# Attention on one core: keys of three head pairs loaded once and copied across the partitions by ScalarE, and the steps on y of branch B moved

## The chip, the cores and the metric

The kernel runs on one core of a Trainium2 chip. Its engines run their own instruction streams and wait for each other by semaphores: the PE (TensorE) multiplies, VectorE (DVE) and ScalarE (ACT) work on tiles element by element, GpSimd (POOL) and SyncE (SP) mostly issue DMAs here. The metric is the device time of one launch in microseconds, as the median of several runs.

## The reference

One layer of an encoder on 1024 tokens with 1024 features, in float32. The change lies in its middle part:

```python
u = rms_norm(h)
qA, kA, vA, qB, kB, vB, gA, gB = split(u @ W_in)
yA = neighbourhood_attention_2d(qA, kA, vA)      # 8 heads of 64, 8 rows x 16 columns around each query
yB = windowed_gqa_sink(rope(qB), rope(kB), vB)   # 8 query heads, 2 key heads, |i - j| <= 128, a sink logit
h = h + (sigmoid(gA) * (yA @ W_A) + sigmoid(gB) * (yB @ W_B)) @ W_out
```

Ahead of it and behind it stands a feed-forward half step of width 2816.

## The kernel before

Products in float32 are made of three matmuls on operands that are split in a high and a low part (`mm3`, L149, L153, L155). The dense products outside the attention work that way and take most of the time.

**The attention loop.** The loop at the end of the trunk goes through 64 units. Units 0 to 31 are branch B: eight blocks of 128 queries, four head pairs each. Units 32 to 63 are branch A: four head pairs `hp`, eight blocks each. The loop is pipelined over iterations n: `scores` of unit n (PE L1631 and L1632, VectorE L1636 adds the bias and takes the row's extreme, ScalarE L1639 takes the exp and the row's sum), `turn` of unit n-2 (transposes on the PE, L1654; ScalarE casts the result to a high part and VectorE subtracts it for the low part, L95 and L98), and `values` of unit n-3 (PE L1668 or L1673, then `write`: L1570 and L1573 for branch B, L1591, L1592, L1596 and L1598 for branch A). Twice in each iteration `filling` takes steps from the generator `filler`: matmuls of the gates (`gate`, copied out of PSUM at L1331 and stored to `g_d`), then the product of branch B's y with W_B (`branch_b`), then products of branch A. So the PE always has dense work between the small matmuls of the units, as long as what both need is there.

**Keys of branch A.** `prep_a(hp)` loads what a head pair needs; it is a generator that the loop drains twice per iteration from n = 23, 33, 41 and 49 on for pairs 0 to 3. K of each head, in a high and a low part, is wanted on both halves of the 128 partitions, and each half is loaded with a DMA of 256 KB on GpSimd's queue (L1303), eight per pair. Then come q (L1306) and v (L1313).

**y of branch B.** The exps are not normalised in the loop. Their sums are collected in `sums_b`; `inverse` (at n = 32) takes the reciprocal, transposes it, copies it out of PSUM (L1355) and writes it to `inv_d` in DRAM (L1356). y goes to DRAM too (`y_d`, one store for four units, L1573). `fetch_y(r0)` loads 128 rows of y (L1368) and calls `fetch_inverse`, which spreads the inverse sums over the partitions with two loads (L1360). `split_y` multiplies both (L1364) and splits the result (L95, L98) for `branch_b`. The dictionary of steps at the end of `filler` says at which step of the last gate each of these happens for the four row blocks.

**Gates of branch B.** `fetch_gate` loads a gate's row block from `g_d` on SyncE's queue (L1477), `open_gate` takes its tanh on ScalarE (L1486).

**What sets the order.** The code names the operations; a scheduler of the framework puts them in an order on each engine by its own estimate of when their inputs are ready, and may put an instruction several units ahead. On the chip each engine keeps that order. Tiles come from rotating buffers (four `raw`, two `xs`, eight `ws`, four banks each of the PSUM pools `d` and `g`), and a load into a buffer waits until its last reader is done.

Of the kernel before, what the change touches and what calls it, by code (L numbers as in the profile page):

```python
# [11 lines left out]
F32R = mybir.dt.float32r  # L12
# [3 lines left out]
P = 128  # L16
# [15 lines left out]
def f32v(ap):  # L32
    return ap.bitcast(F32)
# [3 lines left out]
def trunk_kernel(ctx, tc, x, xt, n1, wg1, wu1, wd1, nm, win, rpb, sink, wa, wb, wout,  # L37
                 n2, wg2, wu2, wd2, nf, c_rope, c_mask_a, c_mask_b, out):
    nc = tc.nc
# [14 lines left out]
    def nm_(s):  # L54
        uid[0] += 1
        return f"{s}_{uid[0]}"
# [12 lines left out]
    def new_fx(k, dt=F32):  # L69
        fx[k] = main.tile([P, 1024], dt, tag=f"fx{k}", bufs=1, name=nm_("fx"))  # L70
        return fx[k]

    def new_ar(g, dt=F32R):
        ar[g] = main.tile([P, 4, 1024], dt, tag=f"ar{g}", bufs=1, name=nm_("ar"))
        return ar[g]

    def slot(k):
        return ar[k // 4][:, k % 4, :]

    def bank(tag):  # L80
        return ps.tile([P, 512], F32, tag=tag, name=nm_(tag))

    def raw4():
        return main.tile([P, 1024], F32, tag="raw", bufs=4, name=nm_("raw"))

    def xs4():
        return main.tile([P, 1024], F32, tag="xs", bufs=2, name=nm_("xs"))
# [6 lines left out]
    def split(dst_hi, dst_lo, src, eng=None, late=False):  # L94
        hi = nc.scalar.copy(dst_hi, src)  # L95
        if late:
            pin(hi)
        (eng or nc.vector).tensor_tensor(dst_lo, src, f32v(dst_hi), op=ALU.subtract)  # L98
# [642 lines left out]
    for h in range(8):  # L741
        for e, f in ((2, bias_fetch), (5, bias_add), (10, bias_put)):
            k = e + 6 * h
# [321 lines left out]
    def by_block(a):  # L1065

        return a.rearrange("p (b j x) -> p j b x", b=NTT, x=16)

    def in_block(a):
        return a.rearrange("p (j b x) -> p j b x", b=NTT, x=16)  # L1070
# [98 lines left out]
    def halves(a):  # L1169
        return a[:HD], a[HD:]  # L1170
# [106 lines left out]
    heads_a = {}  # L1277
# [12 lines left out]
    def prep_a(hp):  # L1290

        slots = [slot(k) for k in ((12, 13, 14, 15, 20, 21) if hp % 2 == 0 else (22, 23, 8, 9, 10, 11))]
        qs, kd, kl = slots[0:2], slots[2:4], slots[4:6]

        def head(k, base, lo):

            r0 = (base + hp) * P + k * HD
            return zs_d[lo][r0:r0 + HD, :]

        for k in range(2):  # L1300
            for lo, dst in enumerate((kd, kl)):
                for a in halves(dst[k]):
                    nc.gpsimd.dma_start(a, head(k, 4, lo))  # L1303
                yield
            for lo in range(2):
                nc.gpsimd.dma_start(halves(qs[k])[k ^ lo], head(k, 0, lo))  # L1306
            yield
        va = [new_fx(k, F32R).rearrange("p (b d) -> p b d", d=P) for k in ((2, 3) if hp % 2 == 0 else (0, 1))]
        for k in range(2):
            src = v_d[hp % 2].rearrange("n t p (j m s x) -> m s j p (n t) x", j=2, m=2, s=2)[hp // 2, k]  # L1310
            dst = f32v(va[k]).rearrange("p (b j) x -> j p b x", j=2)
            for j in range(2):
                (nc.gpsimd if hp > 1 else nc.sync).dma_start(dst[j], src[j])  # L1313
        heads_a[hp] = (qs, kd, kl, va)

    def u_half(c, n):
        h, l = rhs(((B11, T4), (B21, B22))[c // 4][n])
# [16 lines left out]
    Y_B = (4, 5), (6, 7), (16, 17), (18, 19)  # L1334
# [14 lines left out]
    def inverse(t, r0):  # L1349

        n = t.shape[1]
        nc.vector.reciprocal(t, t)
        pt = bank("d")
        nc.tensor.transpose(pt[:n, :P], t, ident)
        nc.scalar.copy(inv_t[:n], pt[:n, :P])  # L1355
        nc.gpsimd.dma_start(inv_d[r0:r0 + n // NTT].rearrange("a (j t) -> (a j) t", t=P), inv_t[:n])  # L1356

    def fetch_inverse(r, r0):
        for s, a in enumerate(halves(r)):
            nc.gpsimd.dma_start(a, inv_d[r0 + s].partition_broadcast(HD))  # L1360
        return r

    def times(a, b):
        nc.vector.tensor_tensor(a, a, b, op=ALU.mult)  # L1364

    def fetch_y(r0):
        mix["y", r0] = raw4()
        nc.gpsimd.dma_start(mix["y", r0], y_d[r0:r0 + P, :])  # L1368
        mix["inv", r0] = fetch_inverse(raw4(), r0 // HD)

    def split_y(slots, r0, eng):

        h, l = [slot(k) for k in slots]
        r = mix.pop(("y", r0))
        times(r, mix.pop(("inv", r0)))
        if r0 < 512:
            r = in_block(r)
            h, l = by_block(h), by_block(l)
        split(h, l, r, eng, True)
# [95 lines left out]
    def fetch_gate(dc):  # L1475
        r = mix["rb", dc] = xs4() if dc % 3 else masks[:, :1024]
        nc.sync.dma_start(r, g_d[D + dc * P:D + (dc + 1) * P, :])  # L1477
# [6 lines left out]
    def open_gate(dc):  # L1484
        r = mix["rb", dc]
        pin(nc.scalar.activation(r, r, AF.Tanh, scale=0.5))  # L1486

    def branch_b():

        for g in (0, 6):  # L1490
            new_ar(g, F32)
        for dc in range(NC8):
            bs = [bank("g") for _ in range(2)]
            mm = branch_mm(bs, mix.pop(("w", dc)), Y_B)
            for c in range(4):
                drain(mm, 1)
                yield
                if c == (0 if dc else 2) and dc + 2 < NC8:
                    fetch_gate(dc + 2)
                if c == 0 and dc == 0:  # L1500
                    split_y(Y_B[3], 3 * P, nc.vector)
                if c == 1 and dc == 0:
                    open_gate(0)
                if c == 0:
                    if dc + 2 < NC8:
                        fetch_w(dc + 2)
                    else:
                        fetch_wa(0, dc + 2 - NC8)
                elif c == 3 and dc + 1 < NC8:
                    open_gate(dc + 1)  # L1510
            rb = mix.pop(("rb", dc))
            for n in range(2):
                sl = slice(n * 512, (n + 1) * 512)
                nc.vector.scalar_tensor_tensor(out=merged(dc)[:, sl], in0=rb[:, sl], scalar=1.0, in1=bs[n],
                                               op0=ALU.add, op1=ALU.mult)
# [14 lines left out]
    def filler():  # L1530
        for dc, nxt in zip(gates, gates[1:] + [None]):
            if nxt is not None:
                yield from gate(dc, {2: lambda: gate_load(gates.index(nxt))})
            else:
                yield from gate(dc, {0: lambda: [fetch_gate(0), fetch_w(0), fetch_w(1)],
                                     1: lambda: [fetch_y(c * P) for c in range(2)],
                                     2: lambda: fetch_y(2 * P),
                                     3: lambda: split_y(Y_B[0], 0, nc.vector),
                                     4: lambda: [split_y(Y_B[1], P, nc.vector), fetch_y(3 * P)],
                                     5: lambda: fetch_gate(1),  # L1540
                                     6: lambda: split_y(Y_B[2], 2 * P, nc.vector)})
        yield from branch_b()
        for k, p in (("P1", 0), ("P5", 0), ("P1", 1), ("P5", 1)):
            a_product(p, k)
            yield
            a_keep(p, k)
            if k == "P1" and p == 1:
                forms_last(0, "P6")
                forms_last(0, "P3")
            if p == 0 and k == "P5":  # L1550
                a_fetch(0)
        a_open(0)
# [139 lines left out]
    for n in range(1 << 30):  # L1692
        got = next(source, None)
        if got is not None:
            scores(got)
        pipe.insert(0, got)
        for hp, n0 in preps.items():
            if n == n0:
                prep = prep_a(hp)
        if prep:  # L1700
            drain(prep, 1)
        filling(n)
        if len(pipe) > 2 and pipe[2] is not None:
            turn(pipe[2])
        if prep:
            drain(prep, 1)
        if n >= 26 and (n - 26) % 8 == 0 and n < 58:
            fetch_bias((n - 26) // 8)
        if n == NTT * 4:
            inverse(sums_b, 0)  # L1710
        elif n in (NTT * 5, NTT * 6, NTT * 7):
            inverse(sums_a[n // NTT - 5], 2 * (n // NTT) - 2)
        if n in (57, 58, 60):
            fetch_ya(min(n - 57, 2))
        if n in (60, 61):
            forms_first(n - 60)
        if n == NTT * 8:
            for k in A_WEIGHTS:
                fetch_wa(*k)
        if n == 63:  # L1720
            times(mix["ya", 2], mix["inv_a", 2])
            form("P2", 0, mix["ya", 2][:, L])
        filling(n)
        if len(pipe) > 3 and pipe[3] is not None:
            values(pipe[3])
        pipe = pipe[:4]
        if not any(pipe):
            break
# [249 lines left out]
```

## Time and profile before

| | us |
|---|---|
| median of 3 runs | 1931.53 |
| lowest and highest run | 1928.98, 1934.27 |
| the profiled run: its own time | 1929.65 |
| the profiled run: its span | 1927.9 |
| mean clock granted to the PE | 0.995 of full speed |

The profile is that of one execution. An engine's line gives its busy time; the waits are idle times of an engine with the instruction that ended them; the chain goes back from the last instruction to what released each. The scores (L1631) stand between 916.6 and 1159.6 us of the span; branch A begins near 1022. Rows are shown in the prediction, where each is used.

### The profile page before, as it was taken

The numbers are of one execution on the slowest core, as the hardware profiler recorded it, in microseconds if no ns is written. First come the engines' busy times: TensorE is split into PE (matmuls) and PEld (weight loads), VectorE is DVE, ScalarE is ACT, GpSimd is POOL, SyncE is SP. The second block draws the span as 40 slices with busy tenths as digits, with TensorE's granted clock in tenths as the row PEclk, the third lists the DMA queues.
The fourth block names the chain that finished last, engine by engine and source line by source line (L and its number), as shares of the span: only waits on it lengthen the run. The fifth ranks groups of instructions, "written<-read, shape, count | busy, mean of one in ns | idle before, by whom it ended". The sixth has DMA issues, their size and how long they took to land.

```text
span 1927.9 us, 26104 instructions
## 1 busy us (share of the span) xinstructions
PE 1905.2 (99%) x9024; PEld 1597.0 (83%) x9024; DVE 1440.5 (75%) x2543; ACT 935.4 (49%) x1824; POOL 252.7 (13%) x471
## 2 busy tenths in 40 slices
PE   9999999999999999999998999999999999999998
PEld 7888888888888888898997888888888888888886
DVE  8988887868957877766776789879676566559664
ACT  7533554544446543445776676265333333344453
POOL 0011322210000112211112310010110001000010
PEclk9999999999999999999999999999999999999999
DMA  6256978887444277865549989653422322493341
GB/s 268 94 186 229 333 274 295 289 292 271 135 148 148 97 235 218 238 217 190 143 129 246 262 239 348 231 207 120 148 103 99 127 88 106 144 362 104 103 143 61
DMA packets 178213, 369.58 MB, mean 192 GB/s; under 512 B 18016, under 2 KB 76304, under 8 KB 178080
## 3 DMA queue, kind: packets, MB, share of 16 engines
q1 hardware_dynamic: 136784, 236.23, 37.1%
q0 software_dynamic: 40432, 130.63, 19.9%
q8 instruction: 71, 1.16, 0.3%
q10 hardware_dynamic: 864, 1.05, 0.2%
q14 instruction: 62, 0.51, 0.1%
HBM read 247.73 MB, written 121.88 MB: 192 GB/s over the span
## 4 chain that ended last, share of the span: by engine, by line
PE 95%; DMA 3%; DVE 1%; ACT 1%; issue 1%; POOL 0%; POOLq 0%; SPq 0%; ACTq 0%; DVEq 0%
PE g L149 17%; PE g L153 17%; PE g L155 17%; PE d L155 12%; PE d L149 12%; PE d L153 12%; PE d L1654 2%; DMA raw<-inv_d 1%; PE g L1673 1%; PE d L1631 1%; PE d L1632 1%; PE d L142 1%; DMA xs<-g_d 1%; PE g L1668 1%; DMA fx<-v_d 0%
## 5 line engine op out<-in xcount | busy, mean ns | idle before, releaser
L149 PE MATMUL g<-ar,ws 128*128 128x512 f32 x1062 | 407.8, 394 | 0.5 <-ACT xs L1331 0.5
L153 PE MATMUL g<-ar,ws 128*128 128x512 f32 x1062 | 404.1, 391 | 0.0
L155 PE MATMUL g<-ar,ws 128*128 128x512 f32 x1062 | 403.0, 391 | 0.0
L153 PE MATMUL d<-ar,ws 128*128 128x512 f32 x706 | 274.9, 389 | 0.6 <-DVE ar L1000 0.6
L149 PE MATMUL d<-ar,ws 128*128 128x512 f32 x706 | 275.3, 390 | 0.0
L155 PE MATMUL d<-ar,ws 128*128 128x512 f32 x706 | 275.0, 389 | 0.0
L155 PEld LDWEIGHTS g<-ar,ws 128*128 128x128 f32 x1062 | 199.8, 188 | 42.1
L153 PEld LDWEIGHTS g<-ar,ws 128*128 128x128 f32 x1062 | 199.7, 188 | 41.4 <-DVE ar L98 0.3
L149 PEld LDWEIGHTS g<-ar,ws 128*128 128x128 f32 x1062 | 196.5, 189 | 36.9 <-ACT xs L1331 0.8
L334 DVE TENSOR_TENSOR ws<-raw,ws 128x512 fp32r<-128x512 f32 x216 | 147.6, 689 | 77.4 <-ACT ws L327 76.5
L327 ACT CAST ws<-raw 128x512 fp32r<-128x512 f32 x216 | 132.7, 620 | 141.8 <-PE g L155 60.8
L153 PEld LDWEIGHTS d<-ar,ws 128*128 128x128 f32 x706 | 132.6, 188 | 28.7 <-DVE ar L1000 1.3
L155 PEld LDWEIGHTS d<-ar,ws 128*128 128x128 f32 x706 | 132.5, 188 | 28.2 <-DVE ws L334 0.8
L149 PEld LDWEIGHTS d<-ar,ws 128*128 128x128 f32 x706 | 132.5, 188 | 27.2
L95 ACT CAST ws<-raw 128x512 fp32r<-128x512 f32 x88 | 54.9, 623 | 116.4 <-PE d L155 61.6
L98 DVE TENSOR_TENSOR ws<-raw,ws 128x512 fp32r<-128x512 f32 x88 | 60.6, 689 | 55.5 <-ACT ws L95 55.5
L446 POOL DMA_DIRECT2D hid<-fx x91 | 49.4, 542 | 344.0 <-DVE fx L506 230.1
L95 ACT CAST ar<-raw 128x512 fp32r<-128x512 f32 (+1 forms) x80 | 52.1, 654 | 82.0 <-PE g L153 51.5
L149 PE MATMUL g<-ws,ws 128*128 128x512 f32 x232 | 90.9, 392 | 0.0
L153 PE MATMUL g<-ws,ws 128*128 128x512 f32 x232 | 90.3, 389 | 0.0
L155 PE MATMUL g<-ws,ws 128*128 128x512 f32 x232 | 90.1, 390 | 0.0
L95 ACT CAST ws<-ar 128x512 fp32r<-128x512 f32 x104 | 64.2, 618 | 47.1 <-PE g L155 25.4
(394 smaller groups left out, 3837.0 us busy)
## 6 DMA issues: line engine op xcount, KB each, us to landing
raw<-hid SPq DMA_DIRECT2D x70, 512.0 KB
hid<-fx POOLq DMA_DIRECT2D x91, 256.0 KB, 2.8
ar<-in_ffn_w_down_dram SPq DMA_DIRECT2D x32, 512.0 KB
raw<-in_ffn_w_up_dram SPq DMA_DIRECT2D x31, 512.0 KB
wo_d<-made POOLq DMA_DIRECT2D x28, 512.0 KB, 4.3
raw<-in_ffn_w_gate_dram SPq DMA_DIRECT2D x27, 512.0 KB
hid<-fa POOLq DMA_DIRECT2D x51, 256.0 KB, 3.0
ar<-zs_d POOLq DMA_DIRECT2D x48, 256.0 KB, 8.0
```

Source lines behind the costliest of these rows:

```text
L95: hi = nc.scalar.copy(dst_hi, src)
L98: (eng or nc.vector).tensor_tensor(dst_lo, src, f32v(dst_hi), op=ALU.subtract)
L142: nc.tensor.transpose(pt[:, c * P:(c + 1) * P], xs[:, (half * 4 + c) * P:(half * 4 + c + 1) * P], ident)
L149: o = nc.tensor.matmul(b, lhs[0], r[0], start=first, stop=False, **kw)
L153: nc.tensor.matmul(b, lhs[0], r[1], start=False, stop=False, **kw)
L155: nc.tensor.matmul(b, lhs[1], r[0], start=False, stop=last, **kw)
L327: nc.scalar.copy(w[0][:, :512], a)
L334: nc.vector.tensor_tensor(w[0][:, 512:], a, f32v(w[0][:, :512]), op=ALU.subtract)
L446: nc.gpsimd.dma_start(hid[PRODUCTS.index(p), i], src)
L1631: nc.tensor.matmul(b[:, :nw], un["q"][s], un["kd"][s][:, k0 * P:k1 * P], start=True, stop=False)
L1632: nc.tensor.matmul(b[:, :nw], un["q"][s], un["kl"][s][:, k0 * P:k1 * P], start=False, stop=True)
L1654: nc.tensor.transpose(pt[:, i * P:(i + 1) * P], un["pr"][s][:, i * P:(i + 1) * P], ident)
```

## The change

Three things change. For head pairs 1 to 3, K is loaded to the first 64 partitions only, and ScalarE copies it to the other 64 (`nc.scalar.copy`, L1322 in the new code); `prep_a` takes its steps in another order, K first, the copies last. The loads of the inverse sums get a function of their own, `fetch_inv`; for row blocks 0 and 1 it is called at n = 32, right behind `inverse`. And the steps on y stand later in the last gate: the splits of blocks 0 and 1 one step, the loads of blocks 2 and 3 two or three steps; the splits of blocks 2 and 3 are in `branch_b`.

```diff
+        copied = hp > 0
         for k in range(2):
             for lo, dst in enumerate((kd, kl)):
-                for a in halves(dst[k]):
+                for a in halves(dst[k])[:1 if copied else 2]:
                     nc.gpsimd.dma_start(a, head(k, 4, lo))
-                yield
+            yield
+        for k in range(2):
             for lo in range(2):
                 nc.gpsimd.dma_start(halves(qs[k])[k ^ lo], head(k, 0, lo))
             yield
...
+        heads_a[hp] = (qs, kd, kl, [new_fx(k, F32R).rearrange("p (b d) -> p b d", d=P) for k in ((2, 3) if hp % 2 == 0 else (0, 1))])
+        yield
+        yield
...
-        heads_a[hp] = (qs, kd, kl, va)
+        yield
+        for k in range(2 if copied else 0):
+            for dst in (kd, kl):
+                yield
+                nc.scalar.copy(halves(dst[k])[1], halves(dst[k])[0])
...
         nc.gpsimd.dma_start(mix["y", r0], y_d[r0:r0 + P, :])
+
+    def fetch_inv(r0):
         mix["inv", r0] = fetch_inverse(raw4(), r0 // HD)
...
-                if c == 0 and dc == 0:
-                    split_y(Y_B[3], 3 * P, nc.vector)
+                if c < 2 and dc == 0:
+                    split_y(Y_B[2 + c], (2 + c) * P, nc.vector)
...
                                      1: lambda: [fetch_y(c * P) for c in range(2)],
-                                     2: lambda: fetch_y(2 * P),
-                                     3: lambda: split_y(Y_B[0], 0, nc.vector),
-                                     4: lambda: [split_y(Y_B[1], P, nc.vector), fetch_y(3 * P)],
-                                     5: lambda: fetch_gate(1),
-                                     6: lambda: split_y(Y_B[2], 2 * P, nc.vector)})
+                                     4: lambda: [split_y(Y_B[0], 0, nc.vector), fetch_inv(2 * P)],
+                                     5: lambda: [split_y(Y_B[1], P, nc.vector), fetch_inv(3 * P), fetch_y(2 * P), fetch_gate(1)],
+                                     6: lambda: fetch_y(3 * P)})
...
         if n == NTT * 4:
             inverse(sums_b, 0)
+            for c in range(2):
+                fetch_inv(c * P)
```

The lines of the new code that are named in rows below are 8 to 10 higher than before. A row is a number, a line and an operation, with the tile written and the tile read; the numbers in tile names only tell tiles apart.

On GpSimd, around the write of the inverse sums of branch B, the order before was this (L1303 and L1306 load K and q of pair 1, L1573 is the last store of branch B's y):

```order
247 L1356 DMA inv_d<-s_867_7677 64x128
248 L1303 DMA ar_5218<-zs_d_3651 64x1024 x2
249 L1306 DMA ar_566<-zs_d_3650 64x1024
250 L1306 DMA ar_566<-zs_d_3651 64x1024
251 L1573 DMA y_d<-xs_9020 64x8x128
252 L1368 DMA raw_9332<-y_d 128x1024
253 L1360 DMA raw_9334<-inv_d 64x1024
254 L1332 DMA g_d<-xs_9260 128x1024
255 L1360 DMA raw_9334<-inv_d 64x1024
256 L1368 DMA raw_9337<-y_d 128x1024
257 L1360 DMA raw_9339<-inv_d 64x1024 x2
```

and with the change (L1364 is the write, L1368 the loads of the inverse, L1581 the store, L1376 the load of y):

```order
248 L1364 DMA inv_d<-s_867_7677 64x128
249 L1308 DMA ar_566<-zs_d_3651 64x1024
250 L1368 DMA raw_9057<-inv_d 64x1024 x2
251 L1368 DMA raw_9060<-inv_d 64x1024 x2
252 L1581 DMA y_d<-xs_9020 64x8x128
253 L1376 DMA raw_9338<-y_d 128x1024
254 L1340 DMA g_d<-xs_9263 128x1024
255 L1376 DMA raw_9340<-y_d 128x1024
256 L1368 DMA raw_9462<-inv_d 64x1024 x2
```

The four loads of the inverse have moved from behind the load of y to ahead of the last store of y, and four loads of K and q that stood between are gone or stand ahead of the write.

On VectorE the first multiply of y with the inverse (L1364) stood here, behind the minima (L1636) of two units:

```order
1418 L1596 TENSOR_TENSOR fa<-g_9239,s_867_7677 64x2x128
1419 L98 TENSOR_TENSOR ws_9272<-d_9274,ws_9272 128x3x128
1420 L98 TENSOR_TENSOR ws_9273<-d_9280,ws_9273 128x3x128
1421 L1592 TENSOR_TENSOR s_867_7677<-g_9286,s_867_7677 64x256
1422 L1636 ISA hs_7682,nmx_9296<-d_9297,fa 128x384
...
1424 L1596 TENSOR_TENSOR fa<-g_9286,s_867_7677 64x2x128
1425 L1636 ISA hs_7683,nmx_9296<-d_9302,fa 128x384
...
1427 L1364 TENSOR_TENSOR raw_9332<-raw_9332,raw_9334 128x1024
```

and stands here with the change (L1372):

```order
1418 L1604 TENSOR_TENSOR fa<-g_9241,s_867_7677 64x2x128
1419 L1372 TENSOR_TENSOR raw_9338<-raw_9338,raw_9057 128x1024
1420 L98 TENSOR_TENSOR ws_9275<-d_9277,ws_9275 128x3x128
1421 L98 TENSOR_TENSOR ws_9276<-d_9283,ws_9276 128x3x128
1422 L1600 TENSOR_TENSOR s_867_7677<-g_9290,s_867_7677 64x256
1423 L1644 ISA hs_7682,nmx_9300<-d_9301,fa 128x384
```

The multiply has moved eight rows forward, ahead of the low parts (L98) of one unit and the minima of the next.

On ScalarE, around the tanh of branch B's gate 2 (L1486), it was:

```order
987 L1591 COPY s_867_7677<-g_9796 64x256
988 L95 CAST ws_9823<-d_9825 128x3x128
989 L1639 ACTIVATE fa,sums_b<-fa,nmx_9806 128x256
990 L95 CAST ws_9824<-d_9831 128x3x128
991 L1639 ACTIVATE fa,sums_b<-fa,nmx_9806 128x256
992 L1591 COPY s_867_7677<-g_9842 64x256
993 L1355 COPY s_867_7677<-d_9838 16x128
994 L95 CAST ws_9871<-d_9873 128x2x128
995 L95 CAST ws_9872<-d_9878 128x2x128
996 L1486 ACTIVATE xs_9718<-xs_9718 128x1024
```

and with the change (L1322 copies K of pair 3, L1496 is the tanh, of gate 3 in `masks` and of gate 2 in `xs`):

```order
995 L1599 COPY s_867_7677<-g_9796 64x256
996 L1322 COPY ar_5218<-ar_5218 64x1024 x2
997 L1647 ACTIVATE fa,sums_b<-fa,nmx_9806 128x256 x2
998 L95 CAST ws_9823<-d_9825 128x3x128
999 L95 CAST ws_9824<-d_9831 128x3x128
1000 L1363 COPY s_867_7677<-d_9838 16x128
1001 L1599 COPY s_867_7677<-g_9842 64x256
1002 L1496 ACTIVATE masks_5701<-masks_5701 128x1024
1003 L1322 COPY ar_5218<-ar_5218 64x1024
1004 L1647 ACTIVATE fa,sums_b<-fa,nmx_9852 128x384
...
1008 L1496 ACTIVATE xs_9717<-xs_9717 128x1024
```

Two copies of K now stand ahead of a unit's exps, a third one unit later, and the tanh of gate 3 stands ahead of that of gate 2.

More of the change, by code (lines that the diff above doesn't have):

```diff
@@ L1307, in prep_a @@
             yield
-        va = [new_fx(k, F32R).rearrange("p (b d) -> p b d", d=P) for k in ((2, 3) if hp % 2 == 0 else (0, 1))]
+        heads_a[hp] = (qs, kd, kl, [new_fx(k, F32R).rearrange("p (b d) -> p b d", d=P) for k in ((2, 3) if hp % 2 == 0 else (0, 1))])
+        yield
+        yield
         for k in range(2):
             src = v_d[hp % 2].rearrange("n t p (j m s x) -> m s j p (n t) x", j=2, m=2, s=2)[hp // 2, k]
-            dst = f32v(va[k]).rearrange("p (b j) x -> j p b x", j=2)
+            dst = f32v(heads_a[hp][3][k]).rearrange("p (b j) x -> j p b x", j=2)
             for j in range(2):
                 (nc.gpsimd if hp > 1 else nc.sync).dma_start(dst[j], src[j])
-        heads_a[hp] = (qs, kd, kl, va)
+        yield
[3 more added lines that the diff above has]
+                nc.scalar.copy(halves(dst[k])[1], halves(dst[k])[0])
     def u_half(c, n):
```

## The prediction

> **What bounds the kernel now.** I read the busy times first, then the waits of the PE, then the stretches around those waits, and last the chain that ended last through them.
>
> ```profile
> PE 1905.2 (99%) x9024; PEld 1597.0 (83%) x9024; DVE 1440.5 (75%) x2543; ACT 935.4 (49%) x1824; POOL 252.7 (13%) x471
> ```
> ```profile
> PE d L1654 <- DVE ws L98: 9.1, 3, 8.5
> PE d L1631 <- DVE nmx L1636: 3.6, 1, 3.6
> ```
>
> The PE is busy for 1905.2 of 1927.9 us, so what a change that leaves its work alone can win is bounded by its waits (total, times, longest). Only two are worth anything, and both lie in the attention loop that the change touches: 8.5 us of transposes waiting for VectorE, and 3.6 us of scores waiting for VectorE. The stretches show what they cost beside the idle time (after the bounds: busy us of PE, PEld, DVE, ACT and POOL with counts, granted clock, DMA share, GB/s):
>
> ```profile
> 1040.00:1060.00 20.00, 11.51 (x63) 10.05 (x62) 9.00 (x26) 7.80 (x22) 5.39 (x10) 0.81 0.87 272
> 1060.00:1080.00 20.00, 19.53 (x111) 17.02 (x110) 17.51 (x43) 13.76 (x35) 8.31 (x16) 0.93 0.89 211
> 1100.00:1120.00 20.00, 16.40 (x93) 14.38 (x92) 12.80 (x37) 11.89 (x33) 7.99 (x15) 0.91 1.19 285
> ```
>
> The clock is below 1 only around the stalls. The chain shows where both come from (start, us, piece):
>
> ```profile
> 1043.73 11.30 DMA raw<-inv_d
> ...
> 1056.86 1.54 PE d L1654 x6
> 1058.40 0.85 PE g L149 x2
> 1059.26 0.85 PE g L153 x2
> 1060.11 0.85 PE g L155 x2
> 1060.96 1.28 PE g L1668 x6
> 1063.03 0.65 PE d L1654 x6
> 1063.68 0.46 PE g L149 x2
> ...
> 1065.18 0.70 PE g L1668 x6
> ...
> 1069.49 0.26 PE d L1631
> ...
> 1092.14 11.87 DMA xs<-g_d
> ...
> 1107.71 0.69 PE d L1631
> ...
> 1108.72 0.85 PE g L149 x2
> ```
>
> **Stall 1** is the multiply of y's first row block by its inverse sums (L1364), which waits for a load of the inverse; the six transposes need the VectorE instruction queued behind it. After it the work at the low clock takes 0.89 (L1654: 1.54 against 0.65), three times 0.39 and 0.58 (L1668) longer, 2.6 us: stall 1 is worth 8.5 + 2.6 = 11.1. **Stall 2** is a tanh of a gate that waits for its load on ScalarE, with exps behind it; 0.43 in the first scores (0.69 against 0.26), 0.39 in the gate's matmuls at 1108.72 and about as much again in those that follow make 1.2, so it is worth 4.8. Both away would be 15.9 us, 0.8%.
>
> **The change, part by part.**
>
> *Stall 1.* The inverse no longer comes after y, but the two blocks' four inverse loads now stand ahead of the last y store on GpSimd's queue, and the load of y needs that store landed.
>
> ```profile
> 1026.93 0.54 POOL L1356 DMA_DIRECT2D inv_d<-s  x1 [3.84 <-ACT s L1355]
> ...
> 1034.52 0.72 POOL L1573 DMA_DIRECT2D y_d<-xs  x1 [4.96 <-DMA fx<-v_d]
> 1042.01 0.59 POOL L1368 DMA_DIRECT2D raw<-y_d  x1 [6.76 <-DMA fx<-v_d]
> ...
> 1044.81 1.03 POOL L1360 DMA_DIRECT2D raw<-inv_d  x2
> ```
>
> The DMA issues, asked for one short stretch each, give the time from issue to landing of the inverse's write, of that y store and of the load of y (KB each, median us last):
>
> ```profile
> inv_d<-s POOLq DMA_DIRECT2D x1, 32.0 KB, 6.4
> ```
> ```profile
> y_d<-xs POOLq DMA_DIRECT2D x1, 256.0 KB, 7.2
> ```
> ```profile
> raw<-y_d POOLq DMA_DIRECT2D x1, 512.0 KB, 7.9
> ```
>
> So: the write lands at 1026.93 + 6.4 = 1033.3; four inverse loads at 0.52 (1.03 for two) are issued by 1035.4, the store then, about 1 us later than now. It stood behind four loads of 256 KB and does so again, so I keep 7.2: landed 1042.6, and y at 7.9 more, 1050.5. Meanwhile VectorE comes to the multiply earlier, because it now stands one unit ahead (the order piece on VectorE):
>
> ```profile
> 1041.63 0.41 DVE L1596 TENSOR_TENSOR fa<-g,s 64x256 f32<-64x256 f32 x1
> ...
> 1055.11 1.23 DVE L1364 TENSOR_TENSOR raw<-raw,raw 128x1024 f32<-128x1024 f32 x1 [9.50 <-DMA raw<-inv_d]
> ```
>
> It is there at 1042.0 and waits 8.5. Today 9.50 of waiting cost the PE 8.5, so 1.0 is covered; then the PE loses 7.5 where it lost 8.5, and the clock falls as before. **Term: -1.0.** What is late next is y itself, not the inverse. Bounds: an earlier store landed in 5.2 and a later load of y in 5.5 (rows below); with both, y is there at 1046.1, the PE loses 3.1 and half of the clock's price: -6.7. With the 8.4 and 9.2 of the K loads below instead, 1053.0, it loses 10.0: +1.5. I take -1.0, from the rows of the same two transfers.
>
> ```profile
> ar<-zs_d POOLq DMA_DIRECT2D x2, 256.0 KB, 8.4
> ...
> y_d<-xs POOLq DMA_DIRECT2D x1, 256.0 KB, 5.2
> ```
> ```profile
> raw<-y_d POOLq DMA_DIRECT2D x1, 512.0 KB, 5.5
> ar<-zs_d POOLq DMA_DIRECT2D x2, 256.0 KB, 6.4
> ```
>
> [...]
>
> *Stall 2.* SyncE now issues the load of gate 2 right behind the load of A's first y (four instructions earlier, past a weight load and two bias loads), and the tanh of gate 3 goes ahead of it. That takes the 4.90 us wait away. **Term: -4.8**, if nothing takes its place on ScalarE at that point. The nearest candidate are the copies.
>
> *Copies.* Twelve of 64x1024 replace twelve loads of 256 KB (3.1 MB). No copy from one half of the partitions to the other is in the trace; the nearest instruction is ScalarE's cast of 1024 columns:
>
> ```profile
> L95 ACT CAST ar<-raw 128x1024 fp32r<-128x1024 f32 x4 | 4.2, 1045 | 0.0
> ```
>
> At 1045 ns they are 12.5 us of an engine that is busy 13.76 of 20 us; bounds are nothing and twice this. Spread over the units of three pairs they are covered by its idle time. The price is the wait for the load: a copy stands in ScalarE's order ahead of exps. The worst place is pair 3, where two copies stand together (the order piece on ScalarE) behind the first row here, on loads that are now issued from 1088.9 (their row last):
>
> ```profile
> 1093.31 0.36 ACT L1591 COPY s<-g 64x256 f32<-64x256 f32 x1
> 1095.02 0.48 ACT L95 CAST ws<-d 128x384 fp32r<-128x384 f32 x1 [1.35 <-PE d L1654]
> ...
> 1104.09 1.06 ACT L1486 ACTIVATE xs<-xs 128x1024 f32<-128x1024 f32 x1 [4.90 <-DMA xs<-g_d]
> ```
> ```profile
> ar<-zs_d POOLq DMA_DIRECT2D x3, 256.0 KB, 9.2
> ```
>
> ScalarE is free at 1093.7 and idle for 1.35 anyway. At 9.2 the first K is there at 1098.1 and the two copies end at 1100.2, which is 5.2 late beyond that idle time; at the 6.4 of the other K row they end at 1097.4, 2.4 late. The tanh's 4.90 cost the PE 3.6, so 1.3 is covered: 1.1 to 3.9. **Term: +2.5**, between the two, since fewer bytes now stand in the queue. For pair 1 the fourth copy waits for a K issued near 1022.0 that lands 8.4 later, at 1030.4, and ScalarE is there near 1028: 2.4, of which 1.3 is covered, about 1; for pair 2 the loads follow the second multiply near 1057, and at 6.4 are in before ScalarE needs them near 1065. **Term: +1.0** for both (0 to +4, if both wait as long as pair 3).
>
> [...] If later exps could pass, the copies' 3.5 us would fall out of the sum and it would be 1924.4 on the profiled run.
>
> *Multiplies 3 and 4.* They stand almost together now, and the load of y's fourth block needs a raw buffer that the split of block 1 frees. That split is done at 1073.2 (the first row), and the fourth multiply is needed about where it is now:
>
> ```profile
> 1072.01 1.22 DVE L98 TENSOR_TENSOR ar<-raw,ar 128x1024 fp32r<-128x1024 f32 x1
> ```
> ```profile
> 1080.22 1.21 DVE L1364 TENSOR_TENSOR raw<-raw,raw 128x1024 f32<-128x1024 f32 x1
> ```
>
> At 5.5 to 7.9 it lands between 1078.7 and 1081.1, with 1.0 covered. **Term: +0.5** (0 to +4, if GpSimd reaches it late behind K loads and the next inverse write).
>
> Sum against the profiled run's own time: 1929.65 - 1.0 - 4.8 + 2.5 + 1.0 + 0.5 = 1927.85. That run is 1.9 below the median of the runs (1931.53), on which the same sum is 1929.7; I forecast **1929**, between the two, nearer to the median. With any one of its terms at a bound it lies between 1924 (stall 1 at -6.7) and 1933 (multiply 4 or the first two pairs' copies at +4) on the median; that is the likeliest case's own range.
>
> **Rivals** (times on the profiled run; 1.9 more on the median).
> - *Both stalls go.* If the store and y land as fast as the fastest rows, or the lighter queue makes them faster, stall 1 is short enough for the clock to stay up, and copies find their K landed: 1929.65 - 11.1 - 4.8 + 2 = 1915.8; with the bound of -6.7 and copies at +1, 1919.2. For it: 3.1 MB fewer in a stretch whose DMA share is 0.87 to 1.19. Against it: 7.2 and 7.9 one after the other behind a store that cannot be issued before 1034.5, and VectorE coming earlier.
> - *ScalarE's queue takes it back.* Copies wait for K in all three pairs, ahead of exps: pair 3 at +3.9, pairs 1 and 2 at +4, multiply 4 at +4, stall 1 at +1.5, against -4.8: 1938.3. It decides from where a K lands more than 1.3 us after ScalarE reaches its copy. For it: K loads of 8.4 to 9.2 us. Against it: fewer transfers ahead of them, and idle ScalarE time in each unit.
> - *The change does not do what it says.* The last store behind the inverse loads makes y as late as the inverse was (+1.5), and the copies stand where the tanh stood (+3.9 against -4.8): 1930.3, no change.
>
> **How the numbers follow.** A measurement of this kernel can tell about 0.3%, 5.8 us, from no change. The forecast has 0.40 and the last rival 0.06, both within 0.3%: 0.46. Both stalls gone, or enough of stall 1: 0.34, faster. ScalarE's queue: 0.20, slower. The range reaches from the first rival to the second, on the median 1917 to 1940; the far ends of both, together about 0.15, are left out.
>
> **What would show it.** Right: the wait of L1654 for VectorE still 6 to 9 us, now ended by the load of y (raw<-y_d) ahead of the first multiply; no wait of 3.6 us at the tanh; ScalarE idle ahead of a copy of K around pair 3. Wrong: the first multiply waiting under 4 us and the clock near 1 in that stretch (first rival), or several waits of the PE for VectorE or ScalarE with copies waiting for K ahead of them (second). Stall 1 is the term to look at first: its y landing at 1046 instead of 1050 alone moves the sum by 5.7.

## The result, and the profile after

| | before | with the change |
|---|---|---|
| median, us | 1931.53 | 1941.97 |
| lowest to highest, us | 1928.98 to 1934.27 | 1939.53 to 1943.85 |
| span of the profiled run, us | 1927.9 | 1937.7 |

The ratio is 1.0054 (95% interval 1.0039 to 1.0069): the change makes the kernel slower by some 10 us. The forecast was 1929 with a range from 1917 to 1940. What came is nearest the second rival, ScalarE's queue, 1.8 us above its price of 1940.2, and not by its sum.

The waits of the PE with the change (total, times, longest):

```profile
PE d L1662 <- DVE ws L98: 9.0, 5, 3.1
PE d L1639 <- ACT s L1363: 4.4, 1, 4.4
PE d L1639 <- DVE nmx L1644: 2.3, 2, 2.0
```

No wait is as long as the 8.5 us of before, but there are more of them, and at or behind the end of each of the four longest (4.4, 3.1, 2.7 and 2.0 us) the clock goes to half for 3.4 us. The stretches (columns as before):

```profile
1020.00:1040.00 20.00, 16.63 (x91) 13.74 (x90) 9.60 (x32) 13.78 (x39) 5.44 (x10) 0.91 0.91 239
1040.00:1060.00 20.00, 16.50 (x91) 14.21 (x89) 11.79 (x32) 11.12 (x30) 3.43 (x6) 0.91 0.86 256
...
1100.00:1120.00 20.00, 14.11 (x71) 11.75 (x70) 9.86 (x28) 15.17 (x34) 5.09 (x8) 0.91 0.89 231
1120.00:1140.00 20.00, 17.68 (x98) 15.04 (x98) 15.54 (x43) 10.92 (x31) 1.66 (x4) 0.91 0.77 224
```

Four stretches of 20 us have a clock of 0.91, where before there were three below 1. What VectorE or ScalarE waited for ahead of them stands in the timelines. ScalarE, its waits for a load around the copies (L1322) and the tanh of a gate (L1496):

```profile
1032.46 1.04 ACT L1322 CAST ar<-ar 64x1024 fp32r<-64x1024 f32 x1 [3.44 <-DMA ar<-zs_d]
...
1100.95 1.04 ACT L1322 CAST ar<-ar 64x1024 fp32r<-64x1024 f32 x1 [3.57 <-DMA ar<-zs_d]
1102.26 1.04 ACT L1322 CAST ar<-ar 64x1024 fp32r<-64x1024 f32 x1 [0.27 <-DMA ar<-zs_d]
1109.27 1.06 ACT L1496 ACTIVATE masks<-masks 128x1024 f32<-128x1024 f32 x1 [3.29 <-DMA masks<-g_d]
```

VectorE, its multiplies of a y with an inverse (L1372):

```profile
1052.33 1.23 DVE L1372 TENSOR_TENSOR raw<-raw,raw 128x1024 f32<-128x1024 f32 x1 [4.11 <-DMA raw<-y_d]
1058.49 1.23 DVE L1372 TENSOR_TENSOR raw<-raw,raw 128x1024 f32<-128x1024 f32 x1 [2.40 <-DMA raw<-y_d]
...
1130.83 1.23 DVE L1372 TENSOR_TENSOR raw<-raw,raw 128x1024 f32<-128x1024 f32 x1 [3.55 <-DMA raw<-y_d]
```

The PE does the same 7872 dense matmuls (L149, L153, L155) in both kernels. So I counted them and compared when the same one starts in the two traces: that shows how late the kernel is, place by place. The places are named by the time in the trace of before; the number is us later (+) or earlier (-) than before. The other kernels of the experiments stand in the same table, since their readings use it.

| kernel | 1020 | 1040 | 1070 | 1090 | 1118 | 1140 | 1180 |
|---|---|---|---|---|---|---|---|
| the change | 0.5 | 6.2 | 0.7 | 3.9 | 7.0 | 10.1 | 9.9 |
| e1 steps only | 0.5 | 0.5 | -4.5 | -4.8 | -9.0 | -3.2 | -3.2 |
| e2 copies only | 0.9 | 6.4 | 1.4 | 3.5 | 9.7 | 7.9 | 8.2 |
| e3 copies in place | 0.5 | 0.4 | -0.6 | 0.3 | 0.2 | 8.0 | 8.2 |
| e4 K twice | 0.2 | 0.3 | -2.2 | -1.2 | -3.8 | -5.0 | -5.0 |
| e5 in place, A late | 0.7 | 0.7 | -1.0 | -0.2 | -2.8 | -3.0 | -0.7 |
| e6 A late | 0.0 | 5.7 | 1.0 | 5.4 | 8.4 | 7.1 | 8.9 |
| e7 pair 1 by DMA | 0.5 | 0.5 | -2.1 | -0.7 | 2.7 | 1.2 | 1.6 |
| e8 K twice, y late | 0.5 | 0.5 | -10.9 | -1.3 | -7.0 | -5.8 | -5.9 |
| e9 all late | 0.4 | 0.4 | -9.7 | -3.1 | -6.4 | -6.5 | -4.3 |
| e10 and y3, y4 later | 1.1 | 1.1 | -8.9 | -2.7 | -7.8 | -7.5 | -5.1 |
| e11 pair 3 by DMA | 0.6 | 6.1 | 0.4 | 3.9 | -1.2 | 4.0 | 4.5 |

From 1020 to 1040 lie pair 1's copies, to 1070 stall 1, to 1090 pair 2's copies and the third and fourth multiply, to 1118 pair 3's copies and stall 2, to 1140 the multiplies of branch A's y. With the change these stages bring +5.7, -5.5, +3.2, +3.1 and +3.1; behind the loop nothing is added. So all of it was lost within 120 us. The PE's order between dense and small matmuls differs between the kernels from about 1063 to 1180: a count of all 9024 matmuls gives the same numbers within 0.6 us at every place but 1090, where it differs by up to 1.5. At 1094 the two counts agree for the change (3.9), e3 (1.1), e5 (0.6) and e7 (0.3), and the stage of the third and fourth multiply is read there below.

### The profile page after: what moved, and what is told of

It reads as the page before. It is cut to its first block, busy times and chain, and to the rows that moved or that the text cites. A ratio compares the mean times of both kernels' runs of the same rounds, so it can differ in the third digit from the quotient of the medians.

```text
span 1937.7 us, 26082 instructions
## 1 busy us (share of the span) xinstructions
PE 1911.0 (99%) x9024; PEld 1599.8 (83%) x9024; DVE 1441.7 (74%) x2543; ACT 948.3 (49%) x1836; POOL 247.2 (13%) x459
## 3 DMA queue, kind: packets, MB, share of 16 engines
q10 hardware_dynamic: 864, 1.05, 0.2%
## 4 chain that ended last, share of the span: by engine, by line
PE 93%; DMA 3%; DVE 2%; ACT 1%; issue 1%; POOL 0%; SPq 0%; POOLq 0%; DVEq 0%; ACTq 0%
PE g L149 17%; PE g L153 17%; PE g L155 17%; PE d L155 12%; PE d L153 12%; PE d L149 12%; PE d L1662 1%; PE g L1681 1%; DMA raw<-y_d 1%; PE d L1639 1%; PE d L1640 1%; DMA masks<-g_d 1%; PE d L142 1%; PE g L1676 0%; DMA y_d<-fa 0%
## 5 line engine op out<-in xcount | busy, mean ns | idle before, releaser
L149 PE MATMUL g<-ar,ws 128*128 128x512 f32 x1062 | 407.8, 395 | 0.6 <-ACT ar L95 0.6
L153 PE MATMUL g<-ar,ws 128*128 128x512 f32 x1062 | 404.5, 392 | 1.3 <-DVE ar L98 1.3
L155 PE MATMUL g<-ar,ws 128*128 128x512 f32 x1062 | 403.5, 391 | 0.0
L149 PE MATMUL d<-ar,ws 128*128 128x512 f32 x706 | 275.3, 390 | 0.0
L153 PE MATMUL d<-ar,ws 128*128 128x512 f32 x706 | 274.8, 389 | 0.2 <-DVE ar L1000 0.2
L155 PE MATMUL d<-ar,ws 128*128 128x512 f32 x706 | 274.9, 389 | 0.1
L153 PEld LDWEIGHTS g<-ar,ws 128*128 128x128 f32 x1062 | 200.1, 189 | 43.4 <-DVE ar L98 2.0
L155 PEld LDWEIGHTS g<-ar,ws 128*128 128x128 f32 x1062 | 200.5, 189 | 42.2
L149 PEld LDWEIGHTS g<-ar,ws 128*128 128x128 f32 x1062 | 196.7, 189 | 37.5 <-ACT ar L95 1.2
L153 PEld LDWEIGHTS d<-ar,ws 128*128 128x128 f32 x706 | 132.5, 188 | 28.1 <-DVE ar L1000 0.6
L155 PEld LDWEIGHTS d<-ar,ws 128*128 128x128 f32 x706 | 132.5, 188 | 27.9 <-DVE ws L334 0.5
L149 PEld LDWEIGHTS d<-ar,ws 128*128 128x128 f32 x706 | 132.6, 188 | 27.3
L98 DVE TENSOR_TENSOR ws<-raw,ws 128x512 fp32r<-128x512 f32 x88 | 60.5, 688 | 54.8 <-ACT ws L95 54.7
L149 PE MATMUL g<-ws,ws 128*128 128x512 f32 x232 | 90.9, 392 | 0.0
L153 PE MATMUL g<-ws,ws 128*128 128x512 f32 x232 | 90.3, 389 | 0.0
L155 PE MATMUL g<-ws,ws 128*128 128x512 f32 x232 | 90.1, 390 | 0.0
```

The source lines that it names most:

```text
L149: o = nc.tensor.matmul(b, lhs[0], r[0], start=first, stop=False, **kw)
L153: nc.tensor.matmul(b, lhs[0], r[1], start=False, stop=False, **kw)
L155: nc.tensor.matmul(b, lhs[1], r[0], start=False, stop=last, **kw)
```

## The experiments

Times are medians; a ratio is to the kernel before on the same chip, with its 95% interval. The median of before was 1931.53 for the change, 1930.82 for e1 to e4, 1930.73 for e5 to e8 and 1931.09 for e9 to e11, so differences between kernels of two such groups are good to about 1 us. The edits are shown against the kernel with the change.

**e1: only the steps on y and the inverse.** `prep_a` is as before.

```diff
-        copied = hp > 0
...
-                for a in halves(dst[k])[:1 if copied else 2]:
+                for a in halves(dst[k]):
...
```

> Only the steps on y and the inverse are moved; K is loaded twice as before, no copies. Theory A (copies that wait for a K load hold ScalarE's exps): with the copies gone the waits of 3.1 us (pair 1) and 4.4 us (pair 3) are gone too, the first multiply waits less than the 9.5 us of before, and the time is 1921 to 1929. Theory B (the moved steps themselves cost: the y store behind the inverse loads, multiplies one unit earlier, the gate's tanh order): 1936 to 1942 here too. Theory C (the copies' own 12.5 us of ScalarE): like A here.

1925.72 us, ratio 0.9976 (0.9963 to 0.9989): half of the change is a gain. Its multiplies (VectorE):

```profile
1051.62 1.22 DVE L1364 TENSOR_TENSOR raw<-raw,raw 128x1024 f32<-128x1024 f32 x1 [4.43 <-DMA raw<-y_d]
...
1126.34 1.22 DVE L1364 TENSOR_TENSOR raw<-raw,raw 128x1024 f32<-128x1024 f32 x1 [5.76 <-DMA raw<-inv_d]
```

Stall 1 still waits, for y and no longer for the inverse, and is about half as long; in the table the kernel is 9.0 us ahead at 1118, so stall 2 is gone as well. It then loses 5.8 at the first multiply of branch A's y, which waits for an inverse.

**e2: only the copies and the new order of `prep_a`.** The steps on y are as before.

```diff
-                if c < 2 and dc == 0:
-                    split_y(Y_B[2 + c], (2 + c) * P, nc.vector)
+                if c == 0 and dc == 0:
+                    split_y(Y_B[3], 3 * P, nc.vector)
...
-            for c in range(2):
-                fetch_inv(c * P)
```

> Only K loaded once and copied by ScalarE, with the new order of the preparation's steps; the steps on y as before. Theory A: the wait of the PE near 1032 us (3.1 us idle, 5.7 with the low clock) and a wait at pair 3 appear, and stall 1 gets shorter only by what the lighter queue gives; 1935 to 1945. Theory B: about as before, 1928 to 1934. Theory C: 1935 to 1945 as well, but with ScalarE busy rather than waiting ahead of the PE's waits.

1935.71 us, ratio 1.0028 (1.0017 to 1.0039). ScalarE waits at the same copies and at the same tanh, that of gate 3:

```profile
1032.50 1.04 ACT L1322 CAST ar<-ar 64x1024 fp32r<-64x1024 f32 x1 [3.13 <-DMA ar<-zs_d]
...
1101.82 1.04 ACT L1322 CAST ar<-ar 64x1024 fp32r<-64x1024 f32 x1 [4.85 <-DMA ar<-zs_d]
...
1112.07 1.06 ACT L1494 ACTIVATE masks<-masks 128x1024 f32<-128x1024 f32 x1 [4.21 <-DMA masks<-g_d]
```

The loss is the copies'. Gain and loss of e1 and e2 add up to nothing (-5.1 and +4.9), yet the whole change loses 10: the two halves do not add, which the next runs explain in part.

**e3: the whole change, the copies kept at their place in the program.** `pin` holds an instruction at its place in the program's order; the copies then stand some 20 to 40 ScalarE instructions later.

```diff
-                nc.scalar.copy(halves(dst[k])[1], halves(dst[k])[0])
+                pin(nc.scalar.copy(halves(dst[k])[1], halves(dst[k])[0]))
```

> The whole change, but each copy is kept at its place in the program (some 25 to 40 ScalarE instructions later) rather than put forward by the scheduler; same number of copies, loads and steps. Theory A: K has landed when ScalarE reaches the copies, no wait of ScalarE for K; pair 1 gives back about 5.7 us and pair 3 at least 4: 1926 to 1934. Theory C (the copies' own time): no change to the whole change, 1938 to 1944. Theory B: 1938 to 1944.

1934.89 us, ratio 1.0027 (1.0016 to 1.0038), 6 to 7 us better than the whole change with the same copies, loads and steps; just above the range that was expected. Had the copies' own time been the cause (theory C), it would have stayed at 1938 to 1944. No copy waits any more, and up to 1118 the kernel is level with before. VectorE's multiplies:

```profile
1052.00 1.22 DVE L1372 TENSOR_TENSOR raw<-raw,raw 128x1024 f32<-128x1024 f32 x1 [9.52 <-DMA raw<-y_d]
...
1096.40 1.23 DVE L1372 TENSOR_TENSOR raw<-raw,raw 128x1024 f32<-128x1024 f32 x1 [2.90 <-DMA raw<-y_d]
...
1125.86 1.22 DVE L1372 TENSOR_TENSOR raw<-raw,raw 128x1024 f32<-128x1024 f32 x1 [6.31 <-DMA raw<-y_d]
```

The first row is stall 1 as the prediction had it (VectorE waits 9.5, the PE 8.2). The last two are new: the multiplies of branch A's first two row blocks. Before they stood on VectorE behind the minima of 57 and 58 units; here they stand behind those of 48 and 54, in the whole change behind 49 and 54. Every kernel here that copies K and lets them go has them forward, and e1, e4 and e8, which load K twice, have them behind 57 and 58; that the scheduler reckons their loads to be there earlier when fewer loads stand ahead is inferred from that. On the chip the load of the second y waits on SyncE for a store of y to land, as the chain of the whole change shows:

```profile
1119.16 7.41 DMA y_d<-fa
1126.58 4.12 DMA raw<-y_d
```

**e4: the whole change, but K loaded twice.** One word differs: `copied = False`.

> The whole change, but K of pairs 1 to 3 is loaded to both halves by DMA and not copied; the new order of the preparation's steps and of the steps on y stays. Theory A: no waits for copies; 1921 to 1932, a little above the kernel with the y steps alone, if the order of the preparation's steps does harm. Theory B: 1936 to 1942. Theory C: 1921 to 1932.

1926.63 us, ratio 0.9979 (0.997 to 0.9989). The twelve copies with all that they bring cost some 15 us: 4.2 faster than before without them, 10.4 slower with them.

**e5: as e3, and branch A's two multiplies at their place as well.**

```diff
-        times(r, mix["inv_a", c])
+        pin(nc.vector.tensor_tensor(r, r, mix["inv_a", c], op=ALU.mult))
```

> The whole change with the copies at their place in the program (as in the third run), and also the two multiplies of branch A's y with their inverse at their place, where the scheduler had put them 10 to 13 units ahead. In the third run these multiplies waited for their y (PE idle 2.2 and 5.5 us, and the low clock behind). Theory D (these multiplies are the rest of what the change costs): 1924 to 1929. Rival: the wait moves to the next user of the same loads or ScalarE is full with the copies: 1931 to 1936.

1928.50 us, ratio 0.9989 (0.998 to 0.9999). That takes some 6 us off e3, as theory D had it; the stage to 1140 costs nothing, though 2.3 are lost behind it. What is left is mostly stall 1:

```profile
PE d L1662 <- DVE nmx L1644: 8.7, 2, 8.0
```

**e6: the whole change with that edit alone.**

> The whole change, copies put forward as they were, only the two multiplies of branch A's y at their place. In the whole change the second of them cost about 2.3 us of idle PE and 3.1 us in all near 1131. Theory D: 1937 to 1940. Rival (what is lost there is lost anyway to the late loads behind pair 3): 1941 to 1943.

1941.00 us, ratio 1.0046 (1.0031 to 1.0061): by the intervals no better than the change, and in the range of the rival. The stage up to 1140 is 4.4 better than in the change, but the stage of pair 2 is 1.2 worse and 1.8 are lost behind 1140. Ahead of it ScalarE waits at the tanh of gate 3 as in the whole change:

```profile
1108.92 1.06 ACT L1496 ACTIVATE masks<-masks 128x1024 f32<-128x1024 f32 x1 [3.44 <-DMA masks<-g_d]
```

**e7: the whole change, pair 1 by DMA.** `copied = hp > 1`.

> The whole change, but pair 1 has its K loaded twice again and not copied; pairs 2 and 3 as in the change. In the whole change the wait at pair 1 made the PE 5.7 us late, and stall 1 behind it cost 5.5 less than before. Theory E (the two are one: whoever is late at the copy waits less for y, so that pair 1's copies are nearly free): 1939 to 1943. Rival (they add): 1935 to 1937.

1933.13 us, ratio 1.0011 (1.0002 to 1.0021), 8 to 9 better: both theories miss. By the table the wait at pair 1 goes (5.7) and stall 1 is longer again, so that at 1070 only 2.8 are won, as the theory has it, though the first multiply stands a unit further back here and so is no like test of it. The rest stands where orders changed with the edit: the third and fourth multiply are a unit apart again (to 1094: +2.4 instead of +3.2), and branch A's multiplies stand behind 51 and 55 units, where they wait for nothing (to 1140: -1.5 instead of +3.1). Pair 3 still waits:

```profile
1097.66 1.04 ACT L1322 CAST ar<-ar 64x1024 fp32r<-64x1024 f32 x1 [2.96 <-DMA ar<-zs_d]
```

**e8: as e4, and branch B's multiplies at their place**, three units later for the first two.

```diff
-        times(r, mix.pop(("inv", r0)))
+        pin(nc.vector.tensor_tensor(r, r, mix.pop(("inv", r0)), op=ALU.mult))
```

> As the fourth run (steps on y moved, new order of the preparation, K loaded twice), but the multiplies of branch B's y with the inverse stay at their place in the program, the first three units later. Theory F (stall 1 is the scheduler's early multiply waiting for y, and nothing needs its result that early): the idle 6.3 us near 1049 and the low clock behind are gone, 1916 to 1921. Rival (the split and the product with W_B wait for y then): 1924 to 1928.

1925.29 us, ratio 0.9966 (0.9953 to 0.9979), by the intervals the same as e4, and in the range of the rival, though it is the third multiply that waits and not the first two. Stall 1 is gone, 10.9 us ahead at 1070, and most of it, 8 to 10 us, is lost again at the third multiply. The wait of the PE, VectorE's row and the issue of that load (median to landing last):

```profile
PE g L149 <- DVE fa L1604: 7.6, 1, 7.6
```
```profile
1081.00 1.22 DVE L1385 TENSOR_TENSOR raw<-raw,raw 128x1024 f32<-128x1024 f32 x1 [6.73 <-DMA raw<-y_d]
```
```profile
raw<-y_d POOLq DMA_DIRECT2D x1, 512.0 KB, 13.4
```

The load of y's third block took 13.4 us; since the second block's, eight loads of K and two of q had been issued on the same queue. The load of the first block took 6.7 in the whole change.

**e9: as e5, and branch B's multiplies at their place** (the edits of e5 and e8).

> The whole change with copies and A's multiplies at their place (as the fifth run), and the multiplies of branch B's y with the inverse at their place too. The fifth run still lost 8.0 us of idle PE near 1046 to the early first multiply; the eighth run lost that nowhere at unit 39 but 7.6 us at the third multiply, behind sixteen K loads on GpSimd's queue. Theory G (with half the K loads the third multiply finds its y): 1917 to 1922, faster than both kernels. Rival (the third multiply waits here too): 1925 to 1929.

1925.77 us, ratio 0.9972 (0.9963 to 0.9982), in the rival's range. The third multiply waits here too, though less:

```profile
1075.19 1.23 DVE L1385 TENSOR_TENSOR raw<-raw,raw 128x1024 f32<-128x1024 f32 x1 [3.92 <-DMA raw<-y_d]
```

**e10: as e9, the splits of y's third and fourth block one step later.**

```diff
-                if c < 2 and dc == 0:
-                    split_y(Y_B[2 + c], (2 + c) * P, nc.vector)
+                if 1 <= c < 3 and dc == 0:
+                    split_y(Y_B[1 + c], (1 + c) * P, nc.vector)
```

> As the ninth run, but the splits of y's third and fourth row block come one step later in the product with W_B. Theory G: the same as the ninth run within 2 us, since nothing waited there. Rival of the ninth run (y's third block is late): 3 to 6 us faster than the ninth run.

1925.39 us, ratio 0.9973 (0.9962 to 0.9984). The same multiply now waits 2.2:

```profile
1076.77 1.22 DVE L1385 TENSOR_TENSOR raw<-raw,raw 128x1024 f32<-128x1024 f32 x1 [2.21 <-DMA raw<-y_d]
```

Its time is that of e9. In e9 the wait had cost something (the rival), but the 2.7 us less of PE idle time (2.3 instead of 5.0) do not show in the median. By the table the stage to 1090 loses 6.2 us in e10 and 6.6 in e9; what takes the place of the shorter wait is not shown.

**e11: the whole change, pair 3 by DMA.** `copied = 0 < hp < 3`.

> The whole change, but pair 3 has its K loaded twice again and not copied; pairs 1 and 2 as in the change. Theory A: the waits at pair 3 (PE idle 4.4 us near 1101 and 1.5 near 1111, with the low clock about 7) go: 1933 to 1937. Rival (the tanh's wait of before or branch A's multiplies, which stay 8 and 3 units ahead of their place, take it back): 1938 to 1942.

1936.61 us, ratio 1.0032 (1.0021 to 1.0043), about 5 better. The stage to 1118 goes from +3.1 to -5.1, so pair 3's copies with the tanh behind them cost 8.2 us there. The edit takes both away: without these copies the scheduler leaves the tanh of gate 3 behind that of gate 2, where it starts at 1118.1 and waits for nothing. 2.1 of the gain are given back in the next stage, at a multiply of branch A that now is reached sooner:

```profile
1128.49 1.23 DVE L1372 TENSOR_TENSOR raw<-raw,raw 128x1024 f32<-128x1024 f32 x1 [5.85 <-DMA raw<-y_d]
```

Kernels e1, e4, e8, e9 and e10 beat both kernels, and e5 just does (its interval ends at 0.9999); the lowest medians, 1925.3 to 1925.8, are of e8, e10, e1 and e9 within half a microsecond, 0.3% below before.

## Why the prediction was wrong, step by step

The sum gave 1927.85 for the profiled run, which took 1939.53, 11.7 more. By the stages of the table the errors are -4.5 at stall 1, +4.7 at pair 1's copies, +2.7 at the third and fourth multiply, +5.4 at stall 2 and pair 3, and +3.1 at branch A's multiplies.

*Stall 1 (predicted -1.0).* The step was right where no copy waited and the first multiply stood at the same place on VectorE, one unit ahead (128 minima belong to 64 units, so the two that it passed are those of one unit and not of two): in e3 VectorE waited 9.5 for y (predicted 8.5), the PE 8.2 (7.5), and the stage brought -1.0. Where the scheduler left the multiply a unit further back, as in e1, the stage brought -5.0. In the whole change it brought -5.5. Pair 1's wait had made VectorE 6.2 us late, so it had less to wait; the last y store came as late (the row below, its wait was for VectorE), but the store and the load of y then took 4.5 and 6.7 instead of the 7.2 and 7.9 that the prediction took. Issued some 4 us earlier, in e3, the store took 8.0.

```profile
1040.70 0.72 POOL L1581 DMA_DIRECT2D y_d<-xs  x1 [3.02 <-DVE xs L1579]
```
```profile
y_d<-xs POOLq DMA_DIRECT2D x1, 256.0 KB, 4.5
```
```profile
raw<-y_d POOLq DMA_DIRECT2D x1, 512.0 KB, 6.7
```

On this queue, with other transfers on it, a load of y took 6.7 with the change, 7.9 before and up to 13.4 in e8.

*Copies of pairs 1 and 2 (predicted +1.0).* The mechanism was right, the size was not: 5.7 at pair 1 alone. The fourth copy waited 3.44, where 2.4 was expected; the working then took off 1.3 as covered, left out the copy's own 1.04, which stands behind the wait, and left out the clock, which fell to 0.91. Idle time of the PE was 3.1 to 3.4 us in that stretch, and the clock was at half for 3.4 us behind it (granted clock 0.50 from 1035.0 to 1038.2), by an estimate 1.7 us of work lost; the last half microsecond or so is open. Together with stall 1 it comes to +0.2 where the prediction had 0.0. That is no merit of the sum: the two errors cancel, because a late VectorE waits less for y (4.11 us in the whole change, 9.52 in e3), which the prediction did not see. e3 shows it from the other side: without pair 1's wait it is 5.8 us ahead of the whole change at 1040 and only 1.3 at 1070.

*Stall 2 and pair 3 (predicted -4.8 + 2.5 = -2.3).* This is the step that failed most: measured +3.1. Stall 2 did go (e1 and e11 are 4.2 and 5.1 ahead in that stage), but pair 3 cost 8.2 and not 2.5. K landed 9.1 us after its issue (median of its first three loads), close to the 9.2 that the prediction set as its worse bound and then moved away from, "since fewer bytes now stand in the queue":

```profile
ar<-zs_d POOLq DMA_DIRECT2D x3, 256.0 KB, 9.1
```

Fewer bytes did not help; why not was not tried. At that bound the term would have been 3.9, so the wait for K is not all. The tanh of gate 3, which the prediction named as going ahead of gate 2's and costed at nothing, waited 3.29 for its own load. And the clock came on top. In the trace of the whole change the PE is idle for 4.4 us behind the first two copies and for 1.5 behind the tanh, and the clock is at half for 3.4 us between them, by an estimate 1.7 lost: 7.6 of the 8.2. No run takes the tanh alone away.

*Multiplies 3 and 4 (predicted +0.5).* Measured +3.2 in the stage, read to 1094, against +1.7 in e3 and +2.4 in e7, where a unit stands between them. None of it is the wait for y that the prediction looked for: neither multiply waits for its load in the whole change. That it is VectorE and ScalarE being full there (two multiplies, pair 2's four copies, splits and a tanh close together) is an inference; no run took one of these alone.

*What the prediction had not got at all.* The multiplies of branch A's y were put forward by 8 and 4 units, the second some 50 us behind the multiplies of branch B that the edit moves, and the prediction has no term for it. Their stage costs 3.1 in the whole change and 7.8 in e3, where the first of them costs 3.0 more in the stage before, by comparison with e5, which takes both away. Out of the whole change alone (e6) the same edit won 4.4 in that stage and next to nothing in the time, so 3.1 is what the stage shows and not what the edit is worth there.

*The rival that came.* ScalarE's queue was named with its place and a price of 1938.3 (1940.2 on the median), and a chance of 0.20. Its sum had +1.5 for stall 1 and +4 for pairs 1 and 2, which came out as -5.5 and +5.7, and it lacked branch A. In the trace of the whole change the exps behind the copies that waited 3.44 and 3.57 start only after them, at 1033.53 and 1103.33, when the copies have ended at 1033.50 and 1103.30. The trace of before showed the same behind the tanh that waited 4.90 (it starts at 1104.09, the first exp behind it at 1105.05), and that should have weighed more.

*What the saved loads were worth.* Fewer K loads by 3.1 MB bring nothing to be seen once no copy waits: e9 and e8 (copies, and K loaded twice) are 1925.8 and 1925.3, though branch A's multiplies stand elsewhere in them.

## What to carry to other kernels

Where an engine keeps its order, as ScalarE did here, an instruction that only moves data, put ahead of work on the critical path, costs what is left of the landing time of its input when the engine reaches it (3.44 us at pair 1, 3.57 at pair 3): price it with the worst landing time seen at that place (9.1 to 9.2 at pair 3), add its own duration (1.04) and the clock (3.4 us at half behind each of these waits), and keep it where its input has long landed. An edit that changes loads can make a scheduler put their consumers forward anywhere behind it, so compare the order over the whole stage and not around the edit. And the stalls of this chain did not add: the wait at pair 1 was partly absorbed by the wait for y behind it (without it e3 was 5.8 us ahead of the whole change at 1040 and 1.3 at 1070), so removing one of two was worth less than its size.

## What the runs showed of the hardware

- A copy of 64 partitions x 1024 on ScalarE took 1.04 to 1.05 us in the whole change, as long as the cast of 128 x 1024 before (1.045): half the partitions saved nothing here.
- An idle time of the PE of 3.1 us was followed by 3.4 us at half the clock, a mean of 0.91 over its 20 us (1020 to 1040), the same as behind one of 3.6 before; after it the kernel was 5.7 us late. The price of these stalls was not their idle time alone. Nor did the time at half the clock grow in step with it: in the whole change 2.0 us (ending at 1132.9) and 4.4 us (ending at 1105.6) were each followed by 3.4 us at half the clock, while 1.0 and 1.5 us (ending at 1060.2 and 1113.0) were followed by none.
- A load of 512 KB on GpSimd's queue took 6.7 us behind a store in the whole change and 13.4 in e8, where ten loads of K and q had been issued ahead of it.
